# The next key tile's transposes ahead of a key tile's value products, and the first triangular inverse on GpSimd, in a hybrid RWKV-7 and attention encoder layer

## The chip, the core and the metric

The kernel runs on one core of a Trainium2 chip. The core has five engines, each with an instruction queue of its own that runs in order: TensorE (PE in the profile; its weight loads are listed apart as PEld), VectorE (DVE), ScalarE (ACT), GpSimd (POOL) and SyncE (SP, which only issues transfers here). All tensors on the chip lie in SBUF, matmul results in PSUM. The metric is the time of one execution on the device in microseconds; the median of several runs counts.

## What is computed

One encoder layer over two requests, 256 and 2048 tokens of width 1024, in fp32. The columns of one input projection go to two groups: an RWKV-7 time mixing (8 heads of 64, run forward and backward) and an attention (8 query heads on 2 key heads, softmax over all keys of the request). Their outputs are joined, projected, and followed by a gated feed-forward part. What matters here:

```python
def wkv7_scan(r, decay, k, v, a_vec, b_vec, reverse):
    ...
        sa = jnp.einsum('bhvk,bhk->bhv', S, a_t)
        S = S * w_t[:, :, None, :] + sa[..., None] * b_t[:, :, None, :] + v_t[..., None] * k_t[:, :, None, :]
        return S, jnp.einsum('bhvk,bhk->bhv', S, r_t)
...
    def block(q_blk):
        s = jnp.einsum('bqhgd,bkhd->bhgqk', q_blk, k).astype(jnp.float32) * scale
        p = jax.nn.softmax(s, axis=-1).astype(v.dtype)
        return jnp.einsum('bhgqk,bkhd->bqhgd', p, v)
```

## The kernel before

**Stages.** The input projection runs over three groups of token chunks. Beside it and up to about 900 us the RWKV operands are made (`e_phase`: decays, keys, values, the products that the scan needs, for six blocks of tokens, four column groups and two directions each). The scan (`scan`) goes over chunks of 64 tokens, and needs for each chunk the inverse of a unit triangular matrix. Attention is a generator that is stepped beside the last operands and then beside the scan (`beside`, with the rates `RATE_E` and `RATE_S`). When both are done, output projection and feed-forward part (`out_ffn`) follow.

**Attention.** It goes over 18 query tiles of 128 tokens for each of the two key heads. `att_scores` makes for each block of 512 keys and each of four heads a score tile on TensorE (L880, L881), its negated maximum on VectorE (`nm`, L882), the exponential on ScalarE (`p`, L884). After the 16 score tiles the factors `f` are made from all maxima and sums on VectorE (L890 to L897), and GpSimd scales each `p` by its factor (L901). `att_values` goes over the key tiles of 128 keys: four transposes into the PSUM tile `at` (L913, two buffers), a split into a high part `pth` (cast on ScalarE, L175) and a low part `ptl` (subtraction on VectorE, L181), and two products with the values into `ao` (L916 with the high part, L917 with the low part). The values of a query tile are stepped while the next one's scores are made.

**Inverses.** `inverses` makes ten inverses, one for each of five groups of chunks and two directions, one after the other in the source; `inv_block` works one out by 31 elimination steps of two tensor products each, L565 and L567, all depending on the one before, on tiles `i` with four buffers, three of which an inverse holds. The engine of the steps is GpSimd for the pairs listed in `INV_POOL` and VectorE for the others. Ahead of them GpSimd clears a tile (L559, L560), behind them VectorE turns the result (the copy L570), and after stores and loads TensorE makes the remaining block (L597, L604). The first two inverses, (0, 0) and (4, 1), are stepped beside the last RWKV operands (`N_EARLY`), and the scan can't begin without them.

**Order.** The source order gives priorities. A scheduler then places the instructions on each engine's queue, so instructions of different generators are interleaved in an order that the source alone doesn't show; the orders of the two kernels are shown below where it matters.

Of the kernel before, what the change touches and what calls it, by code (L numbers as in the profile page):

```python
# [17 lines left out]
P = 128  # L18
# [19 lines left out]
NGROUP = 5  # L38
E_STEPS = 5
N_EARLY = 2  # L40
INV_POOL = ((3, 0), (1, 1), (4, 0), (2, 1))
FF_ORDER = (1, 0, 2)
ATT_ORDER = (6, 7, 8, 9, 10, 11, 0, 1, 2, 3, 4, 5, 12, 13, 14, 15, 16, 17)
RATE_E, RATE_S = 1.0, 2.75
# [52 lines left out]
class Kern:  # L97
# [512 lines left out]
    def inverses(self, sb):  # L610

        self.ready = []
        for bi, d in ((0, 0), (4, 1), (1, 0), (3, 1), (2, 0), (2, 1), (3, 0), (1, 1), (4, 0), (0, 1)):
            eng = self.nc.gpsimd if (bi, d) in INV_POOL else self.nc.vector
            yield from self.inv_block(bi, d, sb, eng)
# [288 lines left out]
    def att_values(self, g, t0, kv, p, sb, ps):  # L904
        nc = self.nc
        act, dve = nc.scalar, nc.vector
        pt, parts, nk = p
        pso = ps.tile([P, 512], F32, name="ao", tag="ao", bufs=1)
        keys = [(i, k) for i in range(len(parts)) for k in range(nk)]
        for i, k in keys:  # L910
            tp = ps.tile([P, 4, P], F32, name="at", tag="at", bufs=2)
            for h in range(4):
                nc.tensor.transpose(tp[:, h, :], pt[h, i][:, k * P:(k + 1) * P], self.ident)  # L913
            hi, lo = self.split(sb, tp.rearrange("p h q -> p (h q)"), [P, 512], "pt", bufs=3)
            lhs = kv[parts[i]][2][:, k].rearrange("p a c -> p (a c)")
            nc.tensor.matmul(pso, lhs, hi, start=(i, k) == keys[0], stop=False)  # L916
            nc.tensor.matmul(pso, lhs, lo, start=False, stop=(i, k) == keys[-1])  # L917
            yield
        o = sb.tile([C, 4, P], F32, name="ov", tag="ov", bufs=2)
        of = o.rearrange("p h q -> p (h q)")  # L920
        act.copy(out=of, in_=pso[64:128])
        dve.tensor_tensor(out=of, in0=pso[0:64], in1=of, op=ALU.add)
        for h in range(4):
            hh = g * 4 + h
            self.st(self.yT[4 + hh // 2][t0 // 768][(hh % 2) * 64:(hh % 2) * 64 + 64, t0 % 768:t0 % 768 + P], o[:, h, :])
# [474 lines left out]
```

## Time and profile before

| | us |
|---|---|
| median of 3 runs | 4082.77 |
| lowest, highest run | 4077.72, 4091.49 |
| profiled execution | 4076.95 |
| its span | 4074.8 |
| TensorE busy | 3880.8 (95%) |
| VectorE busy | 2866.1 (70%) |
| ScalarE busy | 2005.5 (49%) |
| GpSimd busy | 1257.7 (31%) |

The span goes from the first to the last instruction of the profiled execution. Busy times are sums over the span, and stages differ: an engine with a small share can be full in one of them. Idle time is put down to what ended it. In the stages: the input projection up to about 800 us, the last operands with the first scores up to 901, attention with the second inverse up to 1010, scan and attention up to 2226, the last value products up to 2282, then the output projection and feed-forward part.

### The profile page before, as it was taken

What the parts mean: (1) busy time and instruction counts of PE and PEld (TensorE: products, weight loads), DVE (VectorE), ACT (ScalarE), POOL (GpSimd) and SP (SyncE); (2) the same over time, 40 slices, a digit from 0 to 9 for tenths busy, and PEclk for the clock granted to TensorE, in tenths of its full rate; (3) what the DMA queues carried; (4) which work ended last, traced back from release to release, by engine and by line L of the source; (5) the groups of instructions that cost most, each with busy time, mean ns of one, the idle gap of its engine ahead of it and who ended that gap; (6) DMA issues with size and microseconds to landing.
All of it is one profiled execution on the core that took longest, in us unless ns stands there. A gap on an engine that the chain in (4) does not pass through costs nothing.

```text
span 4074.8 us, 71176 instructions
## 1 busy us (share of the span) xinstructions
PE 3880.8 (95%) x26208; PEld 3336.7 (82%) x26208; DVE 2866.1 (70%) x4553; ACT 2005.5 (49%) x3940; POOL 1257.7 (31%) x1776
## 2 busy tenths in 40 slices
PE   8999999979999999999999889999989999999998
PEld 7987878746777777777777689998889988799987
DVE  5478586899889776898887577754477744577643
ACT  4345444456666655656666344443344433344432
POOL 2245353543223556734433122200122200212100
PEclk9999999979999999999999999999999999999999
DMA  6567566662433455444441423243423253422251
GB/s 200 166 204 228 173 207 192 207 165 59 101 74 86 92 120 118 114 109 104 109 111 43 146 86 104 96 181 109 166 93 104 96 184 110 159 87 96 102 181 67
DMA packets 646876, 524.32 MB, mean 129 GB/s; under 512 B 368512, under 2 KB 555520, under 8 KB 646528
## 3 DMA queue, kind: packets, MB, share of 16 engines
q1 hardware_dynamic: 577264, 438.36, 36.2%
q0 software_dynamic: 16944, 68.43, 5.1%
q10 hardware_dynamic: 52320, 12.98, 1.5%
q8 instruction: 207, 3.39, 0.3%
q14 instruction: 141, 1.16, 0.1%
HBM read 355.59 MB, written 166.37 MB: 128 GB/s over the span
## 4 chain that ended last, share of the span: by engine, by line
PE 76%; DVE 9%; DMA 4%; POOL 4%; issue 3%; ACT 3%; SPq 1%; ACTq 0%; DVEq 0%; POOLq 0%
PE acc L1082 23%; PE acc L211 8%; PE acc L212 8%; PE acc L213 8%; PE at L913 5%; PE g L657 3%; PE ao L917 3%; PE ao L916 3%; PE as L880 3%; PE as L881 2%; DVE nm L882 1%; DVE ptl L181 1%; PE hb L705 1%; PE hb L730 1%; PE g L597 1%
## 5 line engine op out<-in xcount | busy, mean ns | idle before, releaser
L1082 PE MATMUL acc<-H,wsh 128*128 128x384 f32 x3168 | 814.6, 337 | 32.6 <-ACT cg L1110 23.0
L1082 PEld LDWEIGHTS acc<-H,wsh 128*128 128x128 f32 x3168 | 578.7, 190 | 36.2 <-ACT cg L1110 24.1
L1082 PE MATMUL acc<-H,wsl 128*128 128x384 f32 x1584 | 533.2, 337 | 0.0
L901 POOL TENSOR_SCALAR p<-p,f 128x512 f32<-128x512 f32 (+1 forms) x528 | 372.8, 728 | 284.8 <-DVE f L897 235.9
L884 ACT ACTIVATE p<-as,nm 128x512 f32<-128x512 f32 (+1 forms) x528 | 360.9, 684 | 162.4 <-DVE nm L882 133.8
L211 PE MATMUL acc<-wsh,H 128*128 128x512 f32 x1080 | 419.8, 391 | 14.6 <-ACT wsh L175 14.6
L212 PE MATMUL acc<-wsl,H 128*128 128x512 f32 x1080 | 420.6, 390 | 0.0
L213 PE MATMUL acc<-wsh,H 128*128 128x512 f32 x1080 | 415.6, 389 | 0.0
L175 ACT CAST pth<-at 128x512 fp32r<-128x512 f32 x520 | 300.1, 586 | 228.7 <-PE at L913 223.2
L181 DVE TENSOR_TENSOR ptl<-at,pth 128x512 fp32r<-128x512 f32 x520 | 353.4, 683 | 75.8 <-ACT pth L175 73.4
L882 DVE TENSOR_REDUCE nm<-as 128x1 f32<-128x512 f32 (+1 forms) x528 | 353.0, 674 | 75.2 <-PE as L881 72.7
L211 PE MATMUL acc<-hThi,wih 128*128 128x384 f32 x1008 | 351.5, 349 | 0.8 <-ACT hThi L175 0.7
L212 PE MATMUL acc<-hTlo,wih 128*128 128x384 f32 x1008 | 348.5, 346 | 0.0
L213 PE MATMUL acc<-hThi,wil 128*128 128x384 f32 x1008 | 348.3, 345 | 0.0
L913 PE MATMUL at<-ident,p 128*128 128x128 f32 x2080 | 326.5, 277 | 2.9 <-POOL p L901 2.5
L913 PEld LDWEIGHTS at<-ident,p 128*128 128x128 f32 x2080 | 262.3, 142 | 68.2 <-POOL p L901 6.1
L181 DVE TENSOR_TENSOR wsl<-wsr,wsh 128x1024 fp32r<-128x1024 f32 x156 | 190.9, 1224 | 170.8 <-ACT wsh L175 170.7
L175 ACT CAST wsh<-wsr 128x1024 fp32r<-128x1024 f32 x156 | 164.1, 1052 | 297.9 <-PE acc L1082 151.8
L1082 PEld LDWEIGHTS acc<-H,wsl 128*128 128x128 f32 x1584 | 300.4, 190 | 0.0
L1025 POOL TENSOR_TENSOR sw<-wsr 128x512 f32<-128x512 f32 x66 | 89.2, 1352 | 643.8 <-DVE wsl L181 552.8
L880 PE MATMUL as<-kh,qs 128*128 128x512 f32 (+1 forms) x528 | 248.4, 471 | 31.8 <-ACT p L884 25.6
L181 DVE TENSOR_TENSOR wsl<-sw,wsh 128x1024 fp32r<-128x1024 f32 x132 | 161.2, 1221 | 138.3 <-ACT wsh L175 138.1
(661 smaller groups left out, 8375.1 us busy)
## 6 DMA issues: line engine op xcount, KB each, us to landing
wsr<-in_ffn_gate SPq DMA_DIRECT2D x66, 512.0 KB, 3.5
wsr<-in_ffn_up SPq DMA_DIRECT2D x66, 512.0 KB, 3.8
wsr<-in_ffn_down SPq DMA_DIRECT2D x66, 512.0 KB, 3.6
wir<-in_w_in POOLq DMA_DIRECT2D x63, 512.0 KB, 4.5
hd<-hid POOLq DMA_DIRECT2D x66, 384.0 KB, 3.8
H<-hd SPq DMA_DIRECT2D x33, 768.0 KB, 6.0
cl<-ard SPq DMA_DIRECT2D x144, 128.0 KB, 2.9
zT<-z SPq DMA_DIRECT2D x84, 192.0 KB, 2.7
```

The source lines that it names most:

```text
L175: nc.scalar.copy(out=hi, in_=src)
L181: e.tensor_tensor(out=lo, in0=src, in1=hi.bitcast(F32), op=ALU.subtract)
L211: mm(out, ahi, bhi, start=first, stop=False)
L212: mm(out, ahi, blo, start=False, stop=False)
L213: mm(out, alo, bhi, start=False, stop=last)
L657: nc.tensor.matmul(psgs[e][:, q, :], bk[rows, q, :], cl[rows, e, q, :], start=True, stop=True)
L880: nc.tensor.matmul(pss[:, :hw], qs[:, h, :], kh, start=True, stop=False)
L882: dve.tensor_reduce(out=nm[:, h, i:i + 1], in_=pss[:, :hw], axis=AX.X, op=ALU.max, negate=True)
L884: act.activation(out=p_[:, :hw], in_=pss[:, :hw], func=AF.Exp, bias=nm[:, h, i:i + 1], accum_out=ls[:, h, i:i + 1])
L901: pool.tensor_scalar(out=t, in0=t, scalar1=f[:, h, i:i + 1], scalar2=1.0, op0=ALU.mult, op1=ALU.mult)
L913: nc.tensor.transpose(tp[:, h, :], pt[h, i][:, k * P:(k + 1) * P], self.ident)
L1082: nc.tensor.matmul(acc, x[l][:, k, :], y_[r][:, k, :], start=first and k == 0 and i == 0, stop=k == 3 and i == 2, skip_group_check=True)
```

## The change

Two edits. The pair (0, 0) is added to `INV_POOL`, so the 62 steps of the first inverse are GpSimd's. And `att_values` makes the transposes and the split of the next key tile (`turned`) ahead of the two products of a key tile; the products are written in one line, L922, for both parts. Buffers and the number of instructions stay as they are.

```diff
--- before.py
+++ after.py
@@ -38,7 +38,7 @@
 NGROUP = 5
 E_STEPS = 5
 N_EARLY = 2
-INV_POOL = ((3, 0), (1, 1), (4, 0), (2, 1))
+INV_POOL = ((0, 0), (3, 0), (1, 1), (4, 0), (2, 1))
 FF_ORDER = (1, 0, 2)
 ATT_ORDER = (6, 7, 8, 9, 10, 11, 0, 1, 2, 3, 4, 5, 12, 13, 14, 15, 16, 17)
 RATE_E, RATE_S = 1.0, 2.75
@@ -907,14 +907,19 @@
         pt, parts, nk = p
         pso = ps.tile([P, 512], F32, name="ao", tag="ao", bufs=1)
         keys = [(i, k) for i in range(len(parts)) for k in range(nk)]
-        for i, k in keys:
+        def turned(i, k):
             tp = ps.tile([P, 4, P], F32, name="at", tag="at", bufs=2)
             for h in range(4):
                 nc.tensor.transpose(tp[:, h, :], pt[h, i][:, k * P:(k + 1) * P], self.ident)
-            hi, lo = self.split(sb, tp.rearrange("p h q -> p (h q)"), [P, 512], "pt", bufs=3)
+            return self.split(sb, tp.rearrange("p h q -> p (h q)"), [P, 512], "pt", bufs=3)
+
+        hl = [turned(*keys[0])]
+        for n, (i, k) in enumerate(keys):
+            if n + 1 < len(keys):
+                hl.append(turned(*keys[n + 1]))
             lhs = kv[parts[i]][2][:, k].rearrange("p a c -> p (a c)")
-            nc.tensor.matmul(pso, lhs, hi, start=(i, k) == keys[0], stop=False)
-            nc.tensor.matmul(pso, lhs, lo, start=False, stop=(i, k) == keys[-1])
+            for m, t in enumerate(hl[n]):
+                nc.tensor.matmul(pso, lhs, t, start=n + m == 0, stop=n + m == len(keys))
             yield
         o = sb.tile([C, 4, P], F32, name="ov", tag="ov", bufs=2)
         of = o.rearrange("p h q -> p (h q)")
```

In the rows of the orders, names stand as out<-in, and the shape behind them is that of the output.

VectorE, around the closing copy L570 of the first inverse, before: `i` are the inverse's tiles, `nm` the maxima of score tiles, `f` the factors of the first query tile's probabilities, `ptl` the low parts of its first key tiles.

```order
L896 RECIPROCAL mx<-mx 128x4
L565 TENSOR_TENSOR i_8697<-i_8693,i_8696 96x31
L897 TENSOR_TENSOR f<-f,mx 128x16
L882 TENSOR_REDUCE nm<-as 128x1
L567 TENSOR_TENSOR i_8696<-i_8696,i_8697 96x31
L882 TENSOR_REDUCE nm<-as 128x1
L570 COPY i_8693<-i_8696 96x1024
L502 TENSOR_TENSOR vs<-pc,vs 128x384
L504 SCALAR_TENSOR_TENSOR vs<-vs,pv,gs 128x384
L882 TENSOR_REDUCE nm<-as 128x1 x2
L181 TENSOR_TENSOR ptl<-at,pth 128x512 x2
```

The same place after:

```order
L472 TENSOR_TENSOR us<-pc,cst 128x384
L570 COPY i_8693<-i_8696 96x1024
L882 TENSOR_REDUCE nm<-as 128x1 x4
L890 TENSOR_REDUCE mx<-nm 128x4
L892 TENSOR_TENSOR f<-mx,nm 128x16
L872 TENSOR_TENSOR qs<-as,qs 64x512
L894 TENSOR_TENSOR ls<-ls,f 128x16
L472 TENSOR_TENSOR us<-pc,cst 128x384
L895 TENSOR_REDUCE mx<-ls 128x4
L896 RECIPROCAL mx<-mx 128x4
L882 TENSOR_REDUCE nm<-as 128x1
L897 TENSOR_TENSOR f<-f,mx 128x16
```

The copy stood behind the factors `f`; now it stands ahead of the first query tile's last four maxima and of the factors, and the steps L565 and L567 are gone from this engine.

GpSimd, from the last step of the RWKV operands (`kd`) to the first scaling of probabilities (`p`), before:

```order
L381 TENSOR_TENSOR kss<-kss,mhalf 128x6
L436 TENSOR_SCALAR kd<-ta,dv 128x384
L444 TENSOR_SCALAR ta<-ta 128x384
L447 TENSOR_TENSOR kd<-kd,ks 128x384
L487 TENSOR_TENSOR kd<-kd 128x384
L901 TENSOR_SCALAR p<-p,f 128x512 x16
```

The same place after, its last rows (the inverse's other steps stand between and ahead of the operands' steps):

```order
L565 TENSOR_TENSOR i_8697<-i_8693,i_8696 96x4x28
L567 TENSOR_TENSOR i_8696<-i_8696,i_8697 96x4x28
L565 TENSOR_TENSOR i_8697<-i_8693,i_8696 96x3x29
L567 TENSOR_TENSOR i_8696<-i_8696,i_8697 96x3x29
L565 TENSOR_TENSOR i_8697<-i_8693,i_8696 96x2x30
L567 TENSOR_TENSOR i_8696<-i_8696,i_8697 96x2x30
L565 TENSOR_TENSOR i_8697<-i_8693,i_8696 96x31
L567 TENSOR_TENSOR i_8696<-i_8696,i_8697 96x31
L901 TENSOR_SCALAR p<-p,f 128x512 x16
```

The scaling L901 stood directly behind the operands' last step; now the steps of the inverse stand between.

TensorE, within the last query tile's values, when the scan is over, before (`at` are the transposed tiles; `pth_28078` and `ptl_28079` come from `at_28073`, and so on by five and six):

```order
L917 MATMUL ao_28039<-ptl_28068,vst1_18414 128x512
L913 MATMUL at_28084<-ident_252,p_27803 128x128
L913 MATMUL at_28084<-ident_252,p_27824 128x128
L913 MATMUL at_28084<-ident_252,p_27841 128x128
L913 MATMUL at_28084<-ident_252,p_27858 128x128
L916 MATMUL ao_28039<-pth_28078,vst1_18414 128x512
L917 MATMUL ao_28039<-ptl_28079,vst1_18414 128x512
L916 MATMUL ao_28039<-pth_28089,vst2_18453 128x512
L913 MATMUL at_28095<-ident_252,p_27803 128x128
L913 MATMUL at_28095<-ident_252,p_27824 128x128
L913 MATMUL at_28095<-ident_252,p_27841 128x128
L913 MATMUL at_28095<-ident_252,p_27858 128x128
```

The same place after (`pth_28065` comes from `at_28060`, `pth_28076` from `at_28071`):

```order
L922 MATMUL ao_28039<-pth_28065,vst1_18423 128x512
L922 MATMUL ao_28039<-ptl_28066,vst1_18423 128x512
L913 MATMUL at_28082<-ident_252,p_27812 128x128
L913 MATMUL at_28082<-ident_252,p_27833 128x128
L913 MATMUL at_28082<-ident_252,p_27850 128x128
L913 MATMUL at_28082<-ident_252,p_27867 128x128
L922 MATMUL ao_28039<-pth_28076,vst1_18423 128x512
L922 MATMUL ao_28039<-ptl_28077,vst1_18423 128x512
L913 MATMUL at_28093<-ident_252,p_27812 128x128
L913 MATMUL at_28093<-ident_252,p_27833 128x128
L913 MATMUL at_28093<-ident_252,p_27850 128x128
L913 MATMUL at_28093<-ident_252,p_27867 128x128
```

The next tile's first product stood between a second product and the transposes behind it; now both products of a tile stand together, and the transposes of the tile after the next follow at once.

## Rows read from the trace of the kernel before

**Rows 1.** Windows by stage: length, busy time of PE, PEld, DVE, ACT, POOL, granted clock.
```profile
815.00:878.00 63.00, 48.04 (x242) 27.21 (x241) 61.55 (x113) 30.03 (x61) 35.35 (x38) 0.60 0.59 166
815.00:901.00 86.00, 64.17 (x327) 35.50 (x325) 83.35 (x169) 41.08 (x89) 36.88 (x41) 0.65 0.55 159
901.00:1010.00 109.00, 98.25 (x527) 73.25 (x527) 98.15 (x203) 74.05 (x180) 49.74 (x70) 0.97 0.36 79
1010.00:2226.00 1216.00, 1173.02 (x11383) 928.63 (x11383) 1004.11 (x1982) 757.21 (x1859) 531.18 (x834) 0.99 0.41 99
2226.00:2282.00 56.00, 48.54 (x237) 33.56 (x235) 39.00 (x70) 32.95 (x70) 25.88 (x36) 0.94 0.10 24
```

**Rows 2.** Window of the inverse's tile i alone: PE, PEld, DVE, POOL busy.
```profile
815.00:901.00 86.00, 0.00 (x0) 0.00 (x0) 24.67 (x63) 0.00 (x0) 0.65 0.55 159
```

**Rows 3.** Chain that ended last, in the tail: start, length, engine, tile, line.
```profile
2265.51 0.50 PE ao L917
2266.01 0.23 PE ao L916
2266.24 0.45 PE at L913 x4
2266.71 0.60 ACT pth L175
2267.33 0.70 DVE ptl L181
2268.08 0.50 PE ao L917
```

**Rows 4.** Waits from 910 to 2290: waiting, releaser, us in total, times, longest.
```profile
PEld as L880 <- ACT p L884: 42.0, 60, 1.9
PEld ao L917 <- DVE ptl L181: 31.4, 53, 2.5
PE ao L917 <- DVE ptl L181: 13.1, 29, 2.2
```

**Rows 5.** VectorE in order of time: start, length, line, out<-in.
```profile
817.38 0.20 DVE L565 TENSOR_TENSOR i<-i,i 96x31 f32<-96x31 f32 x1
...
890.38 0.68 DVE L882 TENSOR_REDUCE nm<-as 128x1 f32<-128x512 f32 x1
...
895.53 0.69 DVE L882 TENSOR_REDUCE nm<-as 128x1 f32<-128x512 f32 x1
896.87 0.16 DVE L890 TENSOR_REDUCE mx<-nm 128x4 f32<-128x16 f32 x1
...
900.73 1.05 DVE L570 COPY i<-i 96x1024 f32<-96x1024 f32 x1
```

**Rows 6.** GpSimd by lines, 1370 to 1425, another inverse there: busy, mean ns, idle before.
```profile
L567 POOL TENSOR_TENSOR i<-i,i 128x31 f32<-128x31 f32 (+15 forms) x31 | 18.0, 580 | 2.4
L565 POOL TENSOR_TENSOR i<-i,i 128x31 f32<-128x31 f32 (+15 forms) x31 | 15.7, 507 | 18.3 <-PE g L597 16.0
```

**Rows 7.** GpSimd in order of time, with the idle time ahead.
```profile
899.48 11.86 POOL L901 TENSOR_SCALAR p<-p,f 128x512 f32<-128x512 f32 x16 [22.26 <-DVE f L897]
```

**Rows 8.** GpSimd and VectorE in order of time, two places where both work at once.
```profile
803.83 1.26 POOL L447 TENSOR_TENSOR kd<-kd,ks 128x512 f32<-128x512 f32 x1
803.90 1.74 DVE L449 TENSOR_TENSOR ta<-ta,kkn 128x512 f32<-128x512 f32 x1 [0.52 <-POOL ta L444]
...
822.08 0.73 POOL L436 TENSOR_SCALAR kd<-ta,dv 128x384 f32<-128x384 f32 x1
822.18 0.25 DVE L567 TENSOR_TENSOR i<-i,i 96x87 f32<-96x87 f32 x1
```

**Rows 9.** VectorE by lines from 815 to 901: busy, mean ns.
```profile
L882 DVE TENSOR_REDUCE nm<-as 128x1 f32<-128x512 f32 x18 | 12.3, 682 | 0.8 <-PE as L881 0.6
L472 DVE TENSOR_TENSOR us<-pc,cst 128x512 f32<-128x512 f32 (+1 forms) x8 | 4.9, 612 | 0.0
...
L449 DVE TENSOR_TENSOR ta<-ta,kkn 128x512 f32<-128x512 f32 x2 | 1.4, 675 | 0.0
```

## The prediction, made before the changed kernel was run

> **What bounds the kernel now.** I read the windows by stage first, then the waits of the stage that the change touches, then single engines in time. TensorE is the bound almost everywhere: from 1010 to 2226 us, where scan and attention run side by side, it is busy for 1173.0 of 1216 us [rows 1]. Two stretches are different. From 815 to 901, where the last RWKV operands are made and the first attention tile is scored, VectorE is busy for 83.35 of 86 us, TensorE for 64.17, and TensorE's granted clock is 0.65 of full speed, a mean of stretches at 1.2 and at 2.4 GHz [rows 1]. There VectorE is the bound, and the first inverse takes 24.67 us of it [rows 2]. From 2226 to 2282 the scan is over and only value products are left; TensorE waits in a loop there [rows 1, 3]. The feed-forward part behind 2308 is not touched. So three places are to be priced: the inverse, the long middle, the tail.
>
> **The transposes in the middle.** In the source a key tile's transposes, split and two value products stood in a row; now the next tile's transposes and split come ahead of the products. But the scheduler had moved them already. Counted in the two orders, 333 of the 520 key tiles had a later tile's transposes ahead of their first value product, and 489 have them now. What counts is how much work lies between a tile's own transposes and its products, since the cast and the subtraction must fit into it: before 17.8 instructions on the average up to the first product and 23.2 up to the second, now 18.3 and 22.8. The instructions are the same kinds in the same number; only their places differ. At the second product (L917), whose operand VectorE makes last, TensorE stood still 13.1 us in all from 910 to 2290, and its weight loads 31.4; at the scores (L880) the weight loads stood 42.0 behind ScalarE's exponentials, which the change doesn't touch [rows 4]. With the distance to the second product half an instruction shorter and the extreme cases fewer, I take 0 for the middle. Bounds: the 13.1 us could shrink by some 8 (187 of 520 tiles had no transposes ahead, 31 have none now, so about 80% of such cases go; of what stands outside the tail that is 8), or the same could be lost where both products now stand together: -8 to +8.
>
> **The tail.** Here the order rules alone. Before, two tiles take 2.57 us: second product 0.50, the other tile's first product 0.23, four transposes 0.45, cast 0.60, subtraction 0.70, and 0.09 between them, until the second product of the next pair starts [rows 3]. In the new order (front: TensorE's last rows) the transposes come directly behind the second product, so the 0.23 drops out of the loop: 2.34 for a pair. TensorE's own work in it is 4 x 0.23 + 2 x 0.45 = 1.82 and VectorE's 2 x 0.70 = 1.40, both below 2.34, so the loop still sets the pace. From 2255 to 2281 nine such pairs stand on the chain: 9 x 0.23 = **2.1 us saved**, and it counts whole, since the feed-forward part waits for the last output.
>
> **The inverse on GpSimd.** VectorE loses 62 steps, 24.67 us less the closing copy of 1.05 that stays [rows 2, 5]. GpSimd gets them. An inverse there costs 18.0 + 15.7 us of records and 2.4 + 2.3 us of gaps between dependent steps (18.3 less the 16.0 that wait for TensorE): 38.4 us [rows 6]. Its own work between 815 and 878 is 35.35 us [rows 1], and nothing follows until 899.48 [rows 7]: there is room, 22 us idle behind 878 and 28 before it. From the first step at 817.4 [rows 5], 35.35 + 38.4 us end at 891.1, if each inverse step found its way free.
>
> It doesn't quite. At 803.83 a GpSimd product of two tensors takes 1.26 us, and the VectorE product beside it 1.74 instead of the 0.68 (mean 675 ns) of its like on 128 x 512 [rows 8, 9]: it ends 0.55 us after GpSimd's, so it stood still meanwhile. But at 822.08 and 822.18 a GpSimd step and a short VectorE step with two inputs run at once, neither drawn out [rows 8]. So two-tensor work of the two engines excludes itself mostly, not always. VectorE's work without the inverse is 83.35 - 24.67 = 58.7 us in this stretch, of which 12.3 (L882) and 4.9 (L472) read PSUM [rows 9]; at most 41 us can stand against GpSimd. If the inverse, 33.7 of GpSimd's 69 us, catches its share of that, 20 us are added and it ends at 911.1. At the other end the waits that GpSimd's own work has today behind VectorE's inverse steps go too; an estimate of 6 us, as that is about what a third of its own two-input waits comes to, VectorE losing that share of such work: 885. I take 897.8, a third of the way from 891.1 to 911.1, since VectorE's load of that kind falls by a third.
>
> The Trainium skill (SBUF — State Buffer, section Who interferes with whom) says that a VectorE instruction with two SBUF inputs and a GpSimd instruction that reads SBUF lock each other out for the whole instruction. The trace agrees at 803.83 and disagrees at 822.08; by the rule alone the end at 911.1 or later would be the likely one, which is the slower rival below.
>
> Who waits for it: the closing copy L570 on VectorE. In the new order it stands ahead of the last four score reductions of the first attention tile and of the softmax factors behind them; before, it stood behind all of them (front: VectorE's rows). So VectorE, which would be there some 20 us earlier, stands still at the copy until GpSimd has finished. Then come the copy, 1.05 [rows 5]; two reductions whose scores are ready, 2 x 0.68 [rows 9]; two more that need their scores first, about 1.3 each as from 890.38 to 895.53 in four steps [rows 5]; and the factors, 896.87 to 899.48, 2.6 [rows 5, 7]: 7.6 us. GpSimd's first scaling of probabilities (L901), which frees the value products, then starts at 905.4 instead of 899.48: 5.9 us later. Two reductions of the second tile more stand ahead of the first value subtraction than before, 2 x 0.68 = 1.4 us done early: **4.5 us lost**. Nothing later gives this back: up to 1010 VectorE is busy 98.15 of 109 us with the second inverse beside the attention [rows 1], and that inverse can't start before the first has given up its buffers. The cover that is gone: before, VectorE ran scores while its inverse stepped along; now it stands still in front of the copy.
>
> **Sum:** 0 - 2.1 + 4.5 = +2.4 us on a profiled execution of 4076.95 us (its span 4074.8): 4079.4. The median of the runs is 5.8 above that execution, which gives 4085.2 against the median of 4082.77. I put it at 4083, between the two, as the three runs lie 14 us apart.
>
> **Rivals.** *Slower: the engines lock each other out.* The inverse ends at 911.1, the first scaling comes at 918.7, 19.2 late; -1.4 - 2.1: +15.7, **4098**. For it: the row at 803.83, and that VectorE's other work has two SBUF inputs nearly throughout. Against it: the row at 822.08. It decides from an end of the inverse at about 907.6, where 2.4 has become 12.2. *Faster: GpSimd hides the inverse and the middle gains.* It ends at 885, the scaling starts at 892.6, 6.9 early; with 1.4, the tail's 2.1 and 8 us of the waits at L917 that is -18.4, **4064**. For it: GpSimd's 50 idle us in the stretch, and VectorE's 97% load before. Against it: the copy's new place, and that the distances to the products hardly moved. *The change does little:* the transposes stood ahead already and one bound takes the other's place; that is the forecast.
>
> **How the numbers follow.** The forecast 0.56, slower 0.24, faster 0.20. About 0.3% (12 us) is what a measurement of this kernel can tell from no change. The forecast lies within it, each rival beyond: faster 0.20, same 0.56, slower 0.24. The range goes to both rivals and some 4 us beyond the slower one, as the runs spread: 4064 to 4103.
>
> **What would show it.** In the profile after: GpSimd's last inverse step between 891 and 905, VectorE idle for 10 us or more in front of the copy behind it, the first L901 a few microseconds later than 899.48; the same idle sums at the second value product (now L922) as at L917; pairs of 2.34 us in the tail. I am wrong if VectorE finds the inverse finished when it comes to the copy (then it is faster), if GpSimd's steps are drawn out to a mean above 0.75 us (slower), or if the middle from 1010 to 2226 moves by more than 8 us either way, for which the orders give no reason.

## The result

The changed kernel takes 4114.06 us (median; 4103.85 to 4121.17) where the kernel before takes 4082.77 beside it: ratio 1.0061, 95% interval 1.0045 to 1.0078. The two medians, of five runs each, lie 31 us apart; the ratio, which takes all runs, says about 25 us slower. The forecast was 4083, the range ended at 4103. The profiled execution is one of 4103.85 us, span 4102.1, so it stands 27 us above the profiled execution of before.

Where the time went, first by stage. The windows of after, in the columns of [rows 1]:

```profile
815.00:878.00 63.00, 43.48 (x172) 24.47 (x171) 54.50 (x68) 26.32 (x52) 56.72 (x76) 0.55 0.63 170
815.00:901.00 86.00, 60.19 (x314) 33.55 (x312) 76.07 (x99) 36.74 (x78) 75.13 (x103) 0.62 0.58 163
901.00:1010.00 109.00, 96.52 (x487) 68.10 (x488) 97.19 (x208) 76.20 (x186) 44.50 (x63) 0.97 0.35 77
1010.00:2226.00 1216.00, 1172.29 (x11157) 922.66 (x11156) 979.92 (x1946) 744.54 (x1814) 526.88 (x828) 0.98 0.41 99
2226.00:2282.00 56.00, 53.20 (x406) 38.88 (x403) 47.06 (x86) 41.57 (x100) 25.78 (x37) 1.00 0.10 27
```

From 815 to 901 VectorE has 70 operations fewer than in [rows 1], and yet is busy only 7.3 us less. From 1010 to 2226 TensorE is "busy" as long as before, 1172.3 us against 1173.0, and gets through 226 matmuls fewer. TensorE's idle time from 910 us to the last value product hardly differs either: 59.4 us before, 59.7 now. So what is lost stands inside the busy time, where matmuls follow one another at longer distances or at the lower clock. The middle can't be read from busy shares; a reader has to compare where the same work stands. The Trainium skill (Perfetto Trace Analysis, section Identifying the Most-Contended Engine) warns of this too: TensorE's matmul occupancy is no measure of how close it is to its limit. The trace agrees; the weight loads' busy time fell from 928.6 us [rows 1] to 922.7 with the same matmul time.

**The inverse.** GpSimd by lines from 815 to 901 (busy, mean ns, idle before), answering [rows 6]:

```profile
L567 POOL TENSOR_TENSOR i<-i,i 96x31 f32<-96x31 f32 (+15 forms) x31 | 23.2, 750 | 1.3
L565 POOL TENSOR_TENSOR i<-i,i 96x31 f32<-96x31 f32 (+15 forms) x31 | 19.9, 640 | 2.8 <-DMA i<-ud 1.3
```

VectorE by lines and shapes in the same stretch, answering [rows 9]:

```profile
L882 DVE TENSOR_REDUCE nm<-as 128x1 f32<-128x512 f32 x14 | 9.4, 680 | 1.1 <-PE as L881 1.0
L449 DVE TENSOR_TENSOR ta<-ta,kkn 128x512 f32<-128x512 f32 x2 | 3.2, 1580 | 1.2 <-POOL ta L444 1.2
L472 DVE TENSOR_TENSOR us<-pc,cst 128x512 f32<-128x512 f32 x4 | 2.7, 678 | 0.0
```

The steps on GpSimd are drawn out from 33.7 us [rows 6] to 43.1. On VectorE the product L449, both of whose operands lie in SBUF, goes from 675 ns [rows 9] to 1580; the reductions L882, which read PSUM, stay at 680. L449 is the extreme case, a mean of two; the other products of two SBUF tiles of 128x512 went from 674 to 676 ns to between 762 (L453) and 896 (L455). So the two engines hold each other up, and in these rows only where VectorE takes two operands from SBUF. The Trainium skill (SBUF — State Buffer, section Who interferes with whom) says that such a VectorE instruction contends with a GpSimd instruction that reads SBUF, and here the trace agrees. Besides, VectorE now waits for GpSimd's own operand steps, which stand between the steps of the inverse: in the stretch it is idle for 9.9 us, where it was for 2.7, and 5.5 of them end at such a step (before, none):

```profile
DVE ta L449 <- POOL ta L444: 4.5, 3, 2.0
```

VectorE and GpSimd where the inverse ends, in order of time:

```profile
897.96 0.54 DVE L472 TENSOR_TENSOR us<-pc,cst 128x384 f32<-128x384 f32 x1
898.64 1.06 DVE L570 COPY i<-i 96x1024 f32<-96x1024 f32 x1
899.63 1.27 DVE L882 TENSOR_REDUCE nm<-as 128x1 f32<-128x512 f32 x2
...
903.33 0.17 DVE L890 TENSOR_REDUCE mx<-nm 128x4 f32<-128x16 f32 x1
```
```profile
898.36 0.25 POOL L567 TENSOR_TENSOR i<-i,i 96x31 f32<-96x31 f32 x1
908.66 1.37 POOL L901 TENSOR_SCALAR p<-p,f 128x512 f32<-128x512 f32 x2 [10.05 <-DVE f L897]
```

The inverse ends at 898.61, and VectorE comes to the copy in that moment, with next to no idle time right ahead of it: it had been slowed to GpSimd's pace. The first scaling L901 starts at 908.66, 9.2 us after [rows 7]. 3.7 us of that stand ahead of the inverse (GpSimd's last operand step L487 ahead of the inverse starts at 815.29 against 811.63, and in most kernels below it lies between 811 and 817), so 5.5 belong to the edit.

**The tail.** The chain at the end, answering [rows 3]:

```profile
2293.47 0.50 PE ao L922
2293.98 0.45 PE at L913 x4
2294.43 0.02 issue
2294.45 0.60 ACT pth L175
2295.05 0.02 issue
2295.07 0.70 DVE ptl L181
2295.77 0.04 issue
2295.82 0.50 PE ao L922
```

A pair takes 2.34 us, the product of the high part is out of the loop.

**The middle.** To compare two orders, every value product is taken as a mark: each kind of TensorE's matmul has one price, fitted over four traces, and the time of a mark plus the price of all that is left behind it is the end that this mark foretells. Foretold end less that of the profiled execution of before, us, and last the real end of the value products:

| kernel | at 960 | 1280 | 1440 | 1480 | 1920 | last product |
|---|---|---|---|---|---|---|
| changed | 7.5 | 3.7 | 11.3 | 22.6 | 23.4 | 25.2 |
| e1_inv | 9.2 | 5.8 | 13.6 | 13.9 | 20.2 | 19.3 |
| e2_turn | 2.8 | -2.0 | 6.4 | 16.4 | 19.9 | 14.9 |
| e3_tail | 0.2 | 4.3 | 3.9 | 4.0 | 10.0 | 7.5 |
| e4_cut | 4.7 | 5.7 | 4.6 | 5.6 | 10.5 | 3.8 |
| e12_turnhoist | 1.2 | -2.2 | -0.3 | 3.3 | 15.3 | 10.4 |

The execution of before, 4076.95 us, is a fast one (its medians lie at 4082.8 to 4090.0), so towards their ends the rows stand some 6 to 13 us too high. e3_tail has the order of the kernel before until the scan is over, so its 10 us at 1920 are this and the scatter of single executions. What stands out of that are two steps. From 1280 to 1440 the changed kernel, e1_inv and e2_turn each fall 7.6 to 8.4 us behind, e3_tail and e4_cut don't; in the changed kernel TensorE's idle time there is 3.9 us (before, 4.2) and 3.4 us more are at the lower clock, so this step stays unexplained. From 1440 to 1480 the changed kernel loses 11.3 us. TensorE there:

```profile
1447.45 0.49 PE L922 MATMUL ao<-ptl,vst 128*128 128x512 f32 x1
1449.74 0.50 PE L880 MATMUL as<-kh,qs 128*128 128x512 f32 x1 [1.80 <-DVE qs L872]
...
1453.01 2.07 PE L657 MATMUL g<-cl,bk__15714 64*128 64x128 f32 x8 [2.07 <-DMA cl<-ard]
```

and the windows from 1440 to 1480, of after and then of before:

```profile
1440.00:1480.00 40.00, 36.13 (x287) 29.43 (x283) 21.82 (x42) 17.35 (x45) 13.91 (x25) 0.79 0.56 113
```
```profile
1440.00:1480.00 40.00, 40.00 (x416) 33.17 (x415) 28.27 (x53) 24.92 (x62) 30.60 (x54) 1.00 0.45 105
```

Two waits of 4 us together (a query tile ends, and its successor's queries aren't ready; then a load of the scan's next chunk isn't there), and behind them the granted clock falls (0.79 is a mean of 2.4 and 1.2 GHz): 287 matmuls in 40 us where before had 416. The two windows hold different work, so the loss is read from the marks, 11.3 us, and not from these counts.

### The profile page after: what moved, and what is told of

It reads as the page before. It is cut to its first block, busy times and chain, and to the rows that moved or that the text cites. A ratio compares the mean times of both kernels' runs of the same rounds, so it can differ in the third digit from the quotient of the medians.

```text
span 4102.1 us, 71152 instructions
## 1 busy us (share of the span) xinstructions
PE 3899.1 (95%) x26208; PEld 3342.4 (81%) x26208; DVE 2855.6 (70%) x4491; ACT 2011.4 (49%) x3940; POOL 1301.9 (32%) x1838
## 3 DMA queue, kind: packets, MB, share of 16 engines
q14 instruction: 141, 1.16, 0.1%
## 4 chain that ended last, share of the span: by engine, by line
PE 73%; DVE 10%; POOL 5%; DMA 5%; issue 4%; ACT 2%; SPq 2%; ACTq 0%; POOLq 0%; DVEq 0%
PE acc L1087 23%; PE acc L211 8%; PE acc L213 8%; PE acc L212 8%; PE ao L922 5%; PE at L913 4%; PE g L657 3%; PE as L880 2%; PE as L881 2%; DVE ptl L181 1%; DVE nm L882 1%; SPq L110 1%; PE hb L705 1%; PE g L597 1%; PE hb L711 1%
## 5 line engine op out<-in xcount | busy, mean ns | idle before, releaser
L901 POOL TENSOR_SCALAR p<-p,f 128x512 f32<-128x512 f32 (+1 forms) x528 | 371.1, 725 | 269.3 <-DVE f L897 192.8
L882 DVE TENSOR_REDUCE nm<-as 128x1 f32<-128x512 f32 (+1 forms) x528 | 352.7, 673 | 67.9 <-PE as L881 66.1
```

What stands on the lines that cost most here:

```text
L882: dve.tensor_reduce(out=nm[:, h, i:i + 1], in_=pss[:, :hw], axis=AX.X, op=ALU.max, negate=True)
L901: pool.tensor_scalar(out=t, in0=t, scalar1=f[:, h, i:i + 1], scalar2=1.0, op0=ALU.mult, op1=ALU.mult)
```

## The experiments

Ratios are to the kernel before on the same chip. "Alternations" counts, in TensorE's order between the first score and the last value product, how often an attention matmul is followed by one of the scan or the inverse; "runs" counts how often the kind of matmul changes at all. Counted in the traces, with every transpose taken as its stage's, alternations are 418 before, 435 in the changed kernel and 524 in e14_cuthoist.

| kernel | median us | ratio (95%) | alternations | runs |
|---|---|---|---|---|
| before | 4082.8 to 4090.0 | 1 | 394 | 3051 |
| changed | 4114.06 | 1.0061 (1.0045 to 1.0078) | 408 | 3175 |
| e1_inv | 4096.59 | 1.0029 (1.0015 to 1.0042) | 399 | 3089 |
| e2_turn | 4099.65 | 1.0033 (1.0020 to 1.0046) | 368 | 3151 |
| e3_tail | 4085.67 | 0.9994 (0.9980 to 1.0008) | 394 | 3051 |
| e4_cut | 4080.41 | 0.9977 (0.9964 to 0.9990) | 399 | 3068 |
| e5_rate | 4097.82 | 1.0018 (1.0002 to 1.0034) | 432 | 3115 |
| e6_copy | 4091.44 | 1.0009 (0.9995 to 1.0023) | 394 | 3086 |
| e7_invcut | 4094.79 | 1.0017 (1.0005 to 1.0029) | 388 | 3056 |
| e8_copyturn | 4096.05 | 1.0018 (1.0001 to 1.0035) | 388 | 3149 |
| e9_copycut | 4102.82 | 1.0032 (1.0020 to 1.0044) | 413 | 3097 |
| e10_rateturn | 4118.74 | 1.0067 (1.0051 to 1.0083) | 437 | 3236 |
| e11_ratecut | 4094.58 | 1.0015 (1.0003 to 1.0027) | 448 | 3130 |
| e12_turnhoist | 4085.42 | 0.9992 (0.9981 to 1.0002) | 388 | 3137 |
| e13_turncl | 4102.00 | 1.0028 (1.0013 to 1.0043) | 439 | 3213 |
| e14_cuthoist | 4139.82 | 1.0124 (1.0103 to 1.0145) | 485 | 3166 |
| e15_hoist | 4088.29 | 0.9999 (0.9984 to 1.0013) | 395 | 3076 |
| e17_cuttail | 4080.01 | 0.9979 (0.9967 to 0.9990) | 399 | 3068 |
| e18_rate270 | 4078.40 | 0.9976 (0.9965 to 0.9987) | 374 | 3013 |
| e19_rate276 | 4085.18 | 0.9990 (0.9977 to 1.0002) | 382 | 3017 |

### Each half alone

e1_inv keeps the first line of the diff, e2_turn the rest of it.

> The kernel before with the list of the inverses on GpSimd changed alone: block (0, 0) is there, and a key tile's transposes stand where they stood. Theory A, the prediction's terms: only the 4.5 us of the inverse, 4087, ratio 1.001; in its trace the first value preparation of the scan comes some 10 to 13 us later than before, and the last value product too. Theory B, the transposes' new order costs the middle: the first value product up to 11 us late, the rest of attention no later than that, 4085 to 4090, ratio 1.001 to 1.002. Theory C, the loss lies in how the scan and attention mesh once the scan starts late: the value products fall behind between 1290 and 1600 as in the changed kernel, the last one some 25 us late, 4105, ratio 1.005 to 1.006.

> The kernel before with the value products' edit alone: the next key tile's transposes stand ahead of a key tile's products, block (0, 0) stays on VectorE. Theory A, the prediction's terms: 2.1 us less at the end and nothing in the middle, 4081, ratio 0.9995; the pairs of the last key tiles 2.34 us each. Theory B, the new order costs the middle: value products take some 0.316 us to the next instruction instead of 0.300, the last one 15 to 20 us late, 4098 to 4103, ratio 1.004 to 1.005. Theory C, only a late start of the scan costs: the last value product within 5 us of the kernel before, 4078 to 4086.

Both lose, 0.29% (12 us) and 0.33% (13.5), and their sum is the whole. Theory A falls for both in size. e2_turn's 4099.65 lies in B's range and outside C's; e1_inv's 4096.59 lies between B and C. In e1_inv 9.2 us are lost by 960, as expected, and some 8 more between 1280 and 1440; e2_turn is not behind at 1280, loses 8.4 to 1440 and 10.0 between 1440 and 1480, at the two waits shown above:

```profile
PE g L657 <- DMA cl<-ard: 2.9, 1, 2.9
PE as L880 <- DVE qs L872: 1.6, 1, 1.6
```

(waits of TensorE in e2_turn from 1444 to 1457: us in total, times, longest).

### The tail alone

```diff
+        last = (g, t0) == (1, ATT_ORDER[-1] * P)
...
+            for m in range(len(hl), min(n + 1 + last, len(keys))):
+                hl.append(turned(*keys[m]))
```

> The kernel before, with the next key tile's transposes ahead of the products for the last query tile alone, which stands behind the end of the scan; every engine's order ahead of it is that of the kernel before. Theory A, the prediction's term of the tail: a pair of key tiles takes 2.34 us instead of 2.57, 2.1 us less in all, 4084 where the kernel before gives 4086. Theory B, the transposes' edit costs wherever it stands: not under 4086, the pairs at 2.57 us or more.

The chain that ended last in e3_tail:

```profile
2276.70 0.50 PE ao L923
...
2279.04 0.51 PE ao L923
...
2281.38 0.50 PE ao L923
```

2.34 us a pair; the time, 0.9994 of before, agrees with 2.1 us and can't be told from none. The tail's term is right in the trace.

### The same borders, the other order in a piece; and no edit of attention at all

A piece is what the attention generator does in one step. In e4_cut the products stand first and the next tile's transposes behind them; in e5_rate nothing but a pacing number is changed.

```diff
-            if n + 1 < len(keys):
-                hl.append(turned(*keys[n + 1]))
             lhs = kv[parts[i]][2][:, k].rearrange("p a c -> p (a c)")
             for m, t in enumerate(hl[n]):
                 nc.tensor.matmul(pso, lhs, t, start=n + m == 0, stop=n + m == len(keys))
+            if n + 1 < len(keys):
+                hl.append(turned(*keys[n + 1]))
```
```diff
-RATE_E, RATE_S = 1.0, 2.75
+RATE_E, RATE_S = 1.0, 2.8
```

> The kernel before with the value products' edit and inside a piece the other order: a key tile's products stand first and the next key tile's transposes behind them, so the program text is in the order of the kernel before, and only the borders of the pieces that are dealt out beside the scan lie elsewhere, as they do in the changed kernel (two key tiles' transposes in a query tile's first piece, products alone in its last). Theory B, transposes ahead of products cost the middle by themselves: this one is back at the kernel before, 4081 to 4090. Theory C, it is where the pieces fall against the scan's waits and the clock that goes with it: it loses as the transposes' edit alone did, 4093 to 4103, with a mean granted clock of 0.971 or less over the runs where the kernel before has 0.9735.

> The kernel before with 2.8 pieces of attention to a step of the scan where it has 2.75: no instruction is added or taken away, 2773 of 21,600 places in the row of TensorE's matmuls hold another one, and attention runs at most 2% ahead. Theory C, the kernel before is at an arrangement that suits the scan's loads and the clock, and any other one loses: 4093 or more, clock 0.972 or less. Theory B, only the transposes' own order and the inverse lose: 4080 to 4090.

e4_cut gains 0.23%, a little more than B allows and far from C; e5_rate loses 0.18% with no edit of the transposes, which speaks for C, but at a mean clock of 0.973, that of the kernel before, where C said 0.972 or less. So neither is enough. From here on a third stood beside them: D, each arrangement of the middle is a draw.

### What the inverse's loss hangs on

e6_copy is e1_inv with the copy L570 on GpSimd for block (0, 0).

> Block (0, 0) of the inverse on GpSimd as in the changed kernel, and the copy behind it on GpSimd too; the transposes stand as before. The prediction's reason for the loss, VectorE stands still at that copy with four score reductions behind it: most of it goes away, the first value preparation of the scan at 900 to 902 us, 4081 to 4088. The rival, the two engines draw each other out while the inverse runs (VectorE's operations of that stretch at 0.77 us each where they took 0.49): the first preparation stays at 906 to 910, 4092 to 4100.

GpSimd in e6_copy:

```profile
897.50 0.25 POOL L567 TENSOR_TENSOR i<-i,i 96x31 f32<-96x31 f32 x1
897.81 2.01 POOL L570 COPY i<-i 96x1024 f32<-96x1024 f32 x1
906.61 4.05 POOL L901 TENSOR_SCALAR p<-p,f 128x512 f32<-128x512 f32 x6 [6.78 <-DVE f L897]
```

The first scaling stays late, at 906.6, with no copy on VectorE to wait at. From L487 to that scaling it takes 92.5 to 95.2 us in the six kernels with the inverse on GpSimd (92.5 to 93.0 where the copy is there too), and 87.0 to 87.9 in the eleven others with the same score stage: 6.3 us between the means, of which the copy's place makes at most 2. For the rest the two engines holding each other up, by the rows above, is the reason left; no run parts it from the waits for GpSimd's operand steps. By the first scaling the rival is right; the time, 4091, lies between the two expectations.

### The order within a piece, on other ground

e8 and e9 are e6_copy with the transposes first and with the products first; e10 and e11 are the kernel before at 2.8 pieces to a step, with the transposes first and with the products first; e7_invcut is the changed kernel with the products first.

> The changed kernel with the copy behind block (0, 0) of the inverse on GpSimd: the inverse there, and transposes ahead of products. Beside it stands e9, the same with products ahead of transposes in a piece. Theory B, transposes ahead of products cost the middle whatever stands around them: this one 15 to 25 us above e9, 4100 to 4112. Theory D, each arrangement of the middle is a draw of some 10 us either way, and the order within a piece decides nothing by itself: the pair within 10 us of each other, or e9 the slower one.

> Block (0, 0) of the inverse and its copy on GpSimd, and in a piece of the value products the products first, the next key tile's transposes behind them. Theory B: the inverse's 2 to 8 us and the 9 us that this order gained without it, 4080 to 4088. Theory D: anywhere from 4080 to 4105.

> The kernel before at 2.8 pieces to a step, and the next key tile's transposes ahead of the products. Theory B: 15 to 25 us above e11, and 10 to 14 above the 4098 of 2.8 pieces alone: 4105 to 4115. Theory D: within 10 us of e11, or below it.

> The kernel before at 2.8 pieces to a step, and in a piece the products ahead of the next key tile's transposes. Theory B: some 9 us below the 4098 of 2.8 pieces alone, 4084 to 4093. Theory D: anywhere from 4080 to 4110.

> The changed kernel (block (0, 0) of the inverse on GpSimd) with the products ahead of the next key tile's transposes in a piece. Theory B: some 23 us under the changed kernel, 4088 to 4092. Theory D: 4085 to 4120.

Transposes first less products first: +23 us at the start (e2_turn less e4_cut), -6 (e8 less e9), +21 (e10 less e11), +18 (changed less e7); each difference is uncertain by some 8 us. B, "whatever stands around them", falls with e8 and e9; D, "decides nothing by itself", fits badly with the other three, which have one sign. The inverse costs much the same where its copy stays on VectorE: 12 us (e1), 11 (changed less e2), 16 (e7 less e4). With the copy on GpSimd it doesn't: +4 (e6), -6 (e8 less e2), +22 (e9 less e4). The two waits near 1450 stand in the changed kernel, e2, e8 and e10, in e10 with

```profile
PE g L657 <- DMA cl<-ard: 2.4, 1, 2.4
PE as L880 <- DVE qs L872: 1.7, 1, 1.7
```

and the foretold end steps up by 7.6 to 11.3 us there; in the others it steps by at most 4.2, but for e14 below with 6.7, which waits 1.3 us for the same load.

### The two waits taken away

e12 makes the queries of the next query tile ahead of the last scores of the one before; e13 has ScalarE issue the scan's loads; e14 and e15 are the first of these edits with products first and on the kernel before.

```diff
+        yield
...
+            scores = [self.att_scores(g, j * P, kv, sb, ps) for j in tiles]
...
+                    if m == (1 if j * P < TP else 13) and n + 1 < len(tiles):
+                        next(scores[n + 1])
```
```diff
-            self.ld(cl[rows, e], ar[:, rows, cs].rearrange("q p t -> p q t"))
+            self.lda(cl[rows, e], ar[:, rows, cs].rearrange("q p t -> p q t"))
```

> The transposes' edit alone, and a query tile's queries are loaded, turned and split three score pieces ahead of the last score of the tile before, so that some 40 of TensorE's matmuls stand between their transposes and the first score that reads them, where 24 did. Theory C, the loss is a meeting of two waits (queries, then the scan's load) and the half clock behind them: the wait for the queries near 1450 us is gone, the 7 to 11 us that were lost from 1440 to 1480 fall under 4, and the time to 4084 to 4093. Theory B, the order itself loses: 4096 to 4103 as without it.

> The transposes' edit alone, and the scan's loads of its decay tiles are issued by ScalarE, where SyncE issued them behind the inverse's stores. Theory C: no wait of 2 us for that load near 1450 us, and 4086 to 4095, less what ScalarE loses by issuing 288 loads at 0.4 us each beside its own 0.6 of the time. Theory B: 4096 or more. If ScalarE's row of work is held up at these loads, all is later: over 4105.

> The queries prepared earlier, as in e12, and in a piece the products ahead of the next key tile's transposes. Theory C: fewer waits for queries, 4072 to 4082. Theory D, every arrangement is a draw: 4075 to 4100.

> The kernel before with the queries prepared earlier, nothing else. Theory C: the waits for queries (5 us in the middle) become fewer, 4080 to 4087. Theory D: 4080 to 4100.

In e12 both waits are gone, the step there is 3.6 us, and the time is back at the kernel before, as theory C said. But its window just behind,

```profile
1480.00:1520.00 40.00, 39.14 (x338) 30.01 (x335) 24.86 (x45) 19.44 (x48) 29.99 (x47) 0.79 0.29 77
```

has the low clock that left the place before it, and the foretold end moves some 10 us later there: a step nearly as large as the changed kernel's, though TensorE waits for 0.7 us in all. So neither the low clock nor the step needs the two waits, and a step in one profiled execution is not yet a difference of the medians. In e13 both waits are gone too (1.4 us for the same load are left just ahead, 0.8 the longest) and the time isn't back: its foretold end is 5.7 us behind at 960 and 21.5 at 1440, so the loss only came earlier. And e14, which C put at 4072 to 4082 and D at 4075 to 4100, takes 4139.82, 51 us more than before, without a new instruction; its long stretch, against 11,383 matmuls at clock 0.99 in [rows 1]:

```profile
1010.00:2226.00 1216.00, 1177.64 (x10749) 914.98 (x10749) 953.54 (x1898) 722.12 (x1764) 512.85 (x808) 0.96 0.40 97
```

With e15 at 0.9999 the earlier queries by themselves do nothing; with e14 the order "products first" loses 54 us to its rival e12, on this fifth ground. C foretold e12's time and that the two waits go; as the whole account it fails with e13 and e14.

### How far a neutral edit goes, and whether a gain stays

e18 and e19 set 2.7 and 2.76 pieces to a step; e17 is e4_cut with the transposes first for the last query tile.

> The kernel before at 2.7 pieces of attention to a step of the scan; 2043 of 21,600 places in TensorE's row hold another matmul. Theory D, an arrangement is a draw: anywhere from 4080 to 4105, and e18 and e19 and the 2.8 of before (4098) differ by 8 us and more. Theory B, only the order of transposes and products counts: within 4 us of the kernel before, 4085 to 4093.

> The kernel before at 2.76 pieces to a step, an edit of 0.4%; 2131 of 21,600 places in TensorE's row hold another matmul, from about the middle of the scan on. Theory D: 4080 to 4105. Theory B: within 4 us of the kernel before.

> Block (0, 0) on VectorE; in a piece the products ahead of the next key tile's transposes, but for the last query tile the transposes ahead of the products. Up to the end of the scan every engine's order is that of the kernel that gained with products first. An arrangement's time belongs to it and comes again, and the tail is worth its 2.1 us: a ratio of 0.996 to 0.998 to the kernel before, 4074 to 4082. If the gain was chance of the measurement: 4084 or more.

e18 gains 0.24%, where 2.8 lost 0.18%: two pacing numbers, 17 us between them and no work changed; e19's 0.10% can't be told from none. B's 4 us fall with e18. e17 repeats e4_cut's gain (0.9979). So an arrangement's time is its own and comes again; it isn't chance of the measurement. e4_cut, e17_cuttail and e18_rate270 beat both kernels.

### What goes along with it

Over the twenty kernels of the table the time goes up with the alternations (correlation 0.70; 0.45 without e14) and with the runs (0.69; 0.78 without e14). One price of an alternation stands in e4_cut:

```profile
1433.37 0.39 PE L881 MATMUL as<-kl,qs 128*128 128x512 f32 x1
1433.60 0.40 PE L880 MATMUL as<-kh,qs 128*128 128x512 f32 x1
1433.93 1.16 PE L657 MATMUL g<-cl,bk__15714 64*128 64x128 f32 x8
1435.01 0.50 PE L920 MATMUL ao<-pth,vst 128*128 128x512 f32 x1
1435.35 0.39 PE L881 MATMUL as<-kl,qs 128*128 128x512 f32 x1
```

From one score matmul to the next it is 0.23 us, from a score matmul to one of the scan 0.33; on the way back the matmul behind the first attention matmul starts 0.34 after it. There and back that is 0.21 us more than without the scan between: for e14's 91 alternations more 19 us of 51, for the changed kernel's 14 more 3. An estimate over all twenty traces (the time of stretches of 200 matmuls from 1010 us on, less the waits, as a sum over kinds, changes of kind and half-clock time) gives 0.49 us for there and back and 0.19 for each other change of kind; by the counts of the traces that makes some 10 us for the changed kernel, 31 for e14 and none for e2_turn. No kernel here changed that count alone, so it is a companion, not a shown cause.

Two others go along less. TensorE's idle time from 910 us to the last value product lies between 49 and 64 us in the twenty traces and has no part in when that product ends (correlation -0.09). The time at 1.2 GHz in the same stretch is 44 us before, 48 in the changed kernel, 61 in e2_turn and 92 in e14; but it is 58 in e3_tail, which has the order of before, so of these four only e14's stands clear of the scatter.

## Why the prediction was wrong

**The middle, 0 with bounds of -8 to +8: the step that failed.** It measured 16 us alone (e2_turn's 13.5 and the tail's 2.1 that it gains), and the forecast's own sign of being wrong, more than 8 us there, came in. The reasoning took the waits that name the value products, and the mean distance between a tile's transposes and its products, and found both unchanged. They were: in the middle TensorE's wait at the second product is even smaller (2.2 us in the changed kernel, 5.8 before). But in e2_turn's trace 8,745 of the 26,208 places in TensorE's row hold a matmul of another kind than before, since attention is dealt out beside a scan, and with them it moved where a query tile ends, where a scan chunk's load falls, and how finely the two kinds of work are cut. So the step from "their waits don't change" to "nothing changes by more than 8 us" was the error: pacing edits that touch none of these instructions moved the time by -10 to +7 us, and other rearrangements of the same work by up to 51. "For which the orders give no reason" was the wrong end to draw from a mean. In e2_turn's profiled execution 10 us stand at one place near 1450, but e12_turnhoist has a step of that size without the two waits and is no slower than before. So what makes this arrangement lose 16 us stays open, and so does why e13, without the two waits, is no faster.

**The inverse, +4.5: the delay came out, its mechanism and its price did not.** Its end at 898.6 was forecast at 897.8, and the first scaling's delay at 5.9 (6.3 measured between groups of kernels). That is in part luck, as the forecast had VectorE stand idle at the copy for 10 us or more. It came there in the same moment, since its own operations with two SBUF operands were drawn out (L449 most, 675 ns to 1580) and it had waited for GpSimd's operand steps. The forecast drew only GpSimd's steps out and left VectorE its old pace. Its row against the lock, 822.08, was misread: GpSimd's step of that form takes 0.66 to 0.67 us in half of its 16 executions and took 0.73 there, so it was drawn out a little; and at 853.78 in the same trace GpSimd's L487 on 128x512, 1.26 us at 811.63, takes 4.80 with six VectorE operations on two SBUF operands beside it. With the copy moved away most of the delay stays (e6_copy). And the edit costs 11 to 16 us on three grounds, where the sum had 4.5: what is lost behind 1010 wasn't in it. The runs with the copy on GpSimd, -6 to +22, suggest that this part is again the arrangement; no run shows it alone.

**The tail, -2.1: right**, in the chain of the changed kernel and of e3_tail, from the order alone.

**The rivals.** None had the middle losing. The slower one had the right sign and the lock, and priced the whole at 15.7 us by an inverse that ends at 911.1; it ended at 898.6. The faster one's end at 885 took 6 us off GpSimd's waits, which no row shows; the steps were drawn out instead.

## What to carry over

Where a generator is dealt out beside another stage and a scheduler orders the whole, an edit of a few lines is two edits: what it says, and a new arrangement of everything beside it. Price the first from its waits, but take the bounds of the second from neutral edits (a pacing number a little up and down), and compare a real edit on several such grounds before believing its sign. Before a step is moved to GpSimd, count what of VectorE's work beside it takes two operands from SBUF: here both engines slowed, not only the new one.

## What was not expected of the hardware

- GpSimd's elimination steps went from 33.7 us [rows 6] to 43.1 beside VectorE's operand work, and a VectorE product of 675 ns to 1580; reductions that read PSUM stayed at 680 ns.
- The lower clock came with waits and without: behind the two waits near 1450 eight scan matmuls took 2.07 us at 1.2 GHz, where they take 1.16 at 2.4 GHz (e4_cut's row above); in e12_turnhoist the mean clock from 1480 to 1520 is 0.79 too, with 0.7 us of waits there.
- From a score matmul to a scan matmul it is 0.33 us, from score to score 0.23; behind the scan, from the first attention matmul to the second, 0.34.
